# Recurrence scores level by level: interleaving, a merged first level, and the order of the steps at the stage roots

## The chip, the cores and the metric

The kernel runs on one core of one Trainium2 chip. Five engines matter here: TensorE (PE, with its weight loads PEld), VectorE (DVE), ScalarE (ACT), the DMA engines, and SyncE (SP), which issues the DMAs. The metric is the device time of one execution in microseconds (us); lower is better. Where several executions of one kernel are known, their median counts.

## The reference, cut to what matters

The model is a two-layer hybrid on one sequence of 256 tokens and 1024 channels, in float32: layer 0 is a gated linear recurrence (HGRN2), layer 1 a sparse attention (NSA), each followed by a SwiGLU feed-forward part. Only the recurrence is touched by the larger part of the change:

```python
def step(state, inp):                      # one chunk of 64 tokens, 8 heads of 128 channels
    q_, k_, v_, g_ = inp
    G = jnp.cumsum(g_, axis=2)             # running sum of log decays
    o_inter = jnp.einsum('bhtk,bhkv->bhtv', q_ * jnp.exp(G), state)
    diff = G[:, :, :, None, :] - G[:, :, None, :, :]
    decay = jnp.where(causal, jnp.exp(jnp.where(causal, diff, 0.0)), 0.0)
    attn = jnp.einsum('bhtk,bhsk,bhtsk->bhts', q_, k_, decay)
    o_intra = jnp.einsum('bhts,bhsv->bhtv', attn, v_)
    ...
    return new_state, o_inter + o_intra
...
o = rms_norm(o, out_norm) * jax.nn.silu(g)
return o @ w_out
```

What is computed per head is a causal 256 x 256 score matrix with a decay for each channel and pair of positions, times the values, then a norm over the head's 128 outputs, a gate, and an output projection.

## The kernel before

Activations lie with channels on the partitions and the 256 tokens along the free axis. Every linear layer is made of three passes on PE: the weight is split into a high and a low half (`wh` by ACT at L321, `wl` by DVE at L325), the activation likewise, and `mm3` multiplies hi by hi, hi by lo and lo by hi (L529 to L531). One *step* in the text below is one such triple of 256 columns. Weights come from HBM in blocks of 1 MB through a ring of four buffers (`raw`, issued on SP in the order of `SCHED`). `process` takes the next block and splits it; `fetch` processes ahead.

The recurrence (`hgrn`) is laid out by the list `ORDER["hgrn"]`. Its heads are handled in four pairs (i = 0 to 3), its tokens in two halves, so there are four (head, half) blocks for each pair. Tokens in `ORDER` are: `D` decays, `i`, `g`, `o` the value, gate and output products, `S` scores, `V` values, `G` and `H` gating, `x` what is left of the products between. A `+` in front makes a product a generator of steps; `S0/4` issues four steps of it behind each block of scores. The order on PE among these is fixed by `issue_after`; all else is ordered by a list scheduler of the tile framework, by program order and by when operands are expected.

- `hgrn_decays` works through eight levels b = 1, 2, 4, ..., 128. At each level ACT copies the operand tile X of the level (L1021 for b = 1, L1023 for the rest; the levels 64 and 128 go to tiles that the trace calls `s`), and DVE multiplies the running decays (L1026, L1028). Level tiles come from one pool of `XBUFS` = 14 buffers, two pairs at a time; the next two pairs' first tiles (L985) need buffers that scores have set free.
- `hgrn_scores` computes for a pair the scores: for each of its four blocks `head_scores` makes 4 diagonal products of 32 columns (L1076), 5 x 4 products of 16 columns for the levels 1 to 16 (L1082), each on a column tile of 128 x 32 of the array into `psl`, and 4 products for the levels 32 and 64 (L1088, L1092) into `psu`. A float32 product is two records in the trace. `psx` (L1049) is the block of the second half against the first. DVE then masks `psl` (L1051, L1058, L1062) and ACT copies `psu` and `psx` (L1065, L1066) into the score tile A.
- `hgrn_values` multiplies A by the values (L1108 to L1110), takes the norm (ACT L1113, then DVE, with small operations), scales (L1129), transposes on PE (L1132) and writes the result over `q` (L1133).
- `ada_pe` (L425) makes the modulation vectors with `raw` as the moving operand, also on column tiles; its result is transposed at L436 from a tile of the tag `m`.
- `stat_end` at the end of each residual (the *root* of the next stage) sums squares on PE (L713), takes a reciprocal root with Newton steps on DVE (L488 to L493), builds a diagonal `dg` (L720) and spreads it over the partitions on PE (`rb`, L722).

PSUM is shared by tags: `acc` with 3 banks, `m` with 4, `ada` with 1.

The order of the recurrence before:

```python
"D0 k i0 g0 S1 i1 +g1 S0/4 x c1 V0 D1 i2 i3 G0 +g2 +g3 +o0 S2/5 S3/5 V1 x H o1 G1 o2 o3"
```

Of the kernel before, what the change touches and what calls it, by code (L numbers as in the profile page):

```python
# [21 lines left out]
P = 128  # L22
# [8 lines left out]
XBUFS = 14  # L31
XMOD, XOFF = 5, 9
WIDE = (1,)
PTS = 3
# [20 lines left out]
def _ada_g(l):  # L55
# [9 lines left out]
        "D0 k i0 g0 S1 i1 +g1 S0/4 x c1 V0 D1 i2 i3 G0 +g2 +g3 +o0 S2/5 S3/5 V1 x H o1 G1 o2 o3"  # L65
# [134 lines left out]
class K:  # L200
# [101 lines left out]
    def process(self):  # L302
# [9 lines left out]
        if kind in ("lin", "half"):  # L312
            ws = []
            for h in range(1 if kind == "half" else 2):
# [10 lines left out]
                nc.vector.tensor_tensor(wl, u, wh.bitcast(F32), op=ALU.subtract)  # L325
# [88 lines left out]
    def ada_pe(self, kind, l, i, t):  # L414
# [19 lines left out]
        pt = self.m_tile([P, 4, P], "adat")  # L434
# [272 lines left out]
    def stat_end(self, ps=None):  # L707
# [11 lines left out]
        for tt in range(2):  # L719
            nc.vector.tensor_scalar_mul(dg[:, tt], self.c("ident"), r[:, tt:tt + 1])  # L720
# [93 lines left out]
    def hgrn(self):  # L814
# [3 lines left out]
        with self.tc.tile_pool(name="hg", bufs=1) as gp, self.tc.tile_pool(name="hg2", bufs=2) as g2:  # L818
# [19 lines left out]
            q = gp.tile([P, 8, S], F32, name="q")  # L838
# [8 lines left out]
            for i in range(4):  # L847
                self.act(q[:, 2 * i:2 * i + 2], pq[i], AF.Silu)
# [40 lines left out]
            def gate_out(n, k, gg, oh, ol):  # L889
                nc.vector.tensor_tensor(gg, q[:, 2 * n:2 * n + 2], gg, op=ALU.mult)  # L890
                self.split(oh[:, k:k + 2, :256], ol[:, k:k + 2, :256], gg)
# [32 lines left out]
            Xs = {}  # L924
            for t in ORDER["hgrn"]:
# [3 lines left out]
                elif t[0] == "D":  # L929
                    Xs.update(self.hgrn_decays(logs if n == 0 else self.hgrn_logs({m: pf[m] for m in (2, 3)}, g2), q, g2))  # L930
                elif t[0] == "S":
                    As[n] = self.hgrn_scores(Xs.pop(n), q[:, 2 * n:2 * n + 2], g2, n, between, int(t[3:] or 0))
                elif t[0] == "+":
                    between = chain(between, {"g": gate_steps, "o": out_steps, "i": value_steps}[t[1]](int(t[2])))
# [13 lines left out]
                elif t[0] == "V":  # L948
                    self.hgrn_values((2 * n, 2 * n + 1), As, v[n], g2, q)
# [44 lines left out]
    def hgrn_decays(self, logs, qs, g2):  # L994
# [16 lines left out]
        for i, rf in rfs.items():  # L1011
            nc.vector.tensor_tensor(rf[:, 0].rearrange("p (h s) -> p h s", h=2), rf[:, 2].rearrange("p (h s) -> p h s", h=2),
                                    qs[:, 2 * i:2 * i + 2], op=ALU.mult)
            nc.vector.tensor_copy(Xs[i][8], rf[:, 1].rearrange("p (h s) -> p h s", h=2))
        for l, b in enumerate(LEVELS):
            n = W // (2 * b)
            for i, rf in rfs.items():
                X = new(i, l)
                if b == 1:
                    odd = [[2, S]]  # L1020
                    nc.scalar.copy(ap(X, 1, *odd), ap(rf, 1, *odd))  # L1021
                else:
                    last = nc.scalar.copy(ap(X, 0, [b, 2], [2 * b, n], [1, b]), ap(rf, W, [b - W, 2], [2 * b, n], [1, b]))  # L1023
# [9 lines left out]
    def hgrn_scores(self, X, q, g2, i, between, fill):  # L1033
# [3 lines left out]

        psl = self.m_tile([P, 4, 112], f"psl{i}")
        psu = self.m_tile([P, 4, P], f"psu{i}")
# [628 lines left out]
```

## Time and profile before

| | |
|---|---|
| runs before (us) | 734.29 median; 733.88, 734.29, 738.5 |
| profiled execution | 736.01 us, of which the span in the trace is 734.2 us |
| PE busy | 712.4 us (97%), 5949 matmul records |
| DVE, ACT busy | 580.3 us (79%), 433.6 us (59%) |
| DMA | 172.49 MB, mean 235 GB/s |
| recurrence with its products | from about 63.5 us (last of the q and f products) to about 184 us (its root) |

The span is what the trace covers; the time of the execution has 1.8 us more around it. In the timeline a row is a run of like instructions: start, length, engine, line, operation, tiles, shape, count, and in brackets how long the engine sat idle before it and what ended that. Matmul lengths overlap, because they are pipelined; what counts for PE is the distance from one start to the next. 256 columns at 128 x 128 in the reduced format start 0.12 us apart.

### The profile page before, as it was taken

The numbers are of one execution on the slowest core, as the hardware profiler recorded it, in microseconds if no ns is written. First come the engines' busy times: TensorE is split into PE (matmuls) and PEld (weight loads), VectorE is DVE, ScalarE is ACT, GpSimd is POOL, SyncE is SP. The second block draws the span as 40 slices with busy tenths as digits, with TensorE's granted clock in tenths as the row PEclk, the third lists the DMA queues.
The fourth block names the chain that finished last, engine by engine and source line by source line (L and its number), as shares of the span: only waits on it lengthen the run. The fifth ranks groups of instructions, "written<-read, shape, count | busy, mean of one in ns | idle before, by whom it ended". The sixth has DMA issues, their size and how long they took to land.

```text
span 734.2 us, 14785 instructions
## 1 busy us (share of the span) xinstructions
PE 712.4 (97%) x5949; PEld 626.6 (85%) x5949; DVE 580.3 (79%) x1177; ACT 433.6 (59%) x849; POOL 0.4 (0%) x5
## 2 busy tenths in 40 slices
PE   7999899999999999999999999999999999999997
PEld 4998688789999999988898897555899888888886
DVE  6997877469999889989589888678689778677651
ACT  5669689347635444534469777558666565655330
POOL 0000000000000000000000000000000000000000
PEclk9999999999999999999999999999999999999999
DMA  8899873823669897988555541654654557556610
GB/s 349 323 370 370 295 285 127 320 81 149 246 232 401 296 363 284 344 314 298 224 191 208 226 170 58 229 205 169 238 192 174 207 203 278 188 214 236 247 69 22
DMA packets 27159, 172.49 MB, mean 235 GB/s; under 512 B 2897, under 2 KB 4305, under 8 KB 7250
## 3 DMA queue, kind: packets, MB, share of 16 engines
q1 hardware_dynamic: 26656, 170.80, 62.7%
q8 instruction: 47, 0.77, 0.4%
q10 hardware_dynamic: 434, 0.74, 0.3%
q14 instruction: 22, 0.18, 0.1%
HBM read 170.48 MB, written 1.05 MB: 234 GB/s over the span
## 4 chain that ended last, share of the span: by engine, by line
PE 81%; ACT 7%; DVE 5%; DMA 4%; issue 1%; SPq 0%; ACTq 0%
PE ffo L541 11%; PE ff L530 6%; PE ff L529 6%; PE ff L531 6%; PE ffo L542 6%; PE ff L541 5%; DMA raw<-in_w 3%; PE po L1546 3%; PE ff L542 2%; PE adapsss L425 2%; ACT wh L321 2%; PE ptt L1529 2%; PE s L1489 2%; DVE wl L325 1%; PE nso L529 1%
## 5 line engine op out<-in xcount | busy, mean ns | idle before, releaser
L321 ACT CAST wh<-raw 128x1024 fp32r<-128x1024 f32 x199 | 207.4, 1048 | 170.2 <-PE ffo L541 48.6
L325 DVE TENSOR_TENSOR wl<-raw,wh 128x1024 fp32r<-128x1024 f32 x199 | 242.0, 1221 | 68.8 <-ACT wh L321 68.3
L541 PE MATMUL ffo<-g,wh 128*128 128x512 f32 x352 | 123.6, 394 | 0.0
L542 PE MATMUL ffo<-g,wl 128*128 128x256 f32 x352 | 99.1, 282 | 0.0
L531 PE MATMUL ff<-hh,wl 128*128 128x256 f32 (+1 forms) x352 | 99.1, 282 | 0.0
L530 PE MATMUL ff<-hl,wh 128*128 128x256 f32 (+1 forms) x352 | 98.8, 282 | 0.0
L529 PE MATMUL ff<-hh,wh 128*128 128x256 f32 (+1 forms) x352 | 98.6, 282 | 0.0
L541 PEld LDWEIGHTS ffo<-g,wh 128*128 128x128 f32 x352 | 66.1, 188 | 15.4
L387 DVE CUSTOM_DVE_ANT_0 junk<-raw,crep 128x1024 f32<-128x1024 f32 x64 | 77.9, 1218 | 1.8 <-DMA raw<-in_w 1.6
L531 PEld LDWEIGHTS ff<-hh,wl 128*128 128x128 f32 x352 | 66.5, 189 | 0.0
L530 PEld LDWEIGHTS ff<-hl,wh 128*128 128x128 f32 x352 | 66.3, 189 | 0.1
L529 PEld LDWEIGHTS ff<-hh,wh 128*128 128x128 f32 x352 | 66.1, 189 | 0.2 <-ACT hh L731 0.2
L542 PEld LDWEIGHTS ffo<-g,wl 128*128 128x128 f32 x352 | 66.1, 188 | 0.0
L541 PE MATMUL ff<-h,wh 128*128 128x512 f32 x152 | 54.0, 394 | 0.0
L542 PE MATMUL ff<-h,wl 128*128 128x256 f32 x152 | 42.6, 281 | 0.0
L541 PEld LDWEIGHTS ff<-h,wh 128*128 128x128 f32 x152 | 28.7, 189 | 6.5
L463 ACT ACTIVATE Pt<-Pt,nm 128x128 f32<-128x128 f32 x64 | 28.2, 442 | 8.1 <-DVE nm L1498 7.9
L794 DVE SCALAR_TENSOR_TENSOR x<-ffo,mod,x 128x256 f32<-128x256 f32 x32 | 15.4, 481 | 19.6 <-PE ffo L542 19.2
L542 PEld LDWEIGHTS ff<-h,wl 128*128 128x128 f32 x152 | 28.6, 188 | 0.0
L524 ACT CAST g<-fg 128x256 fp32r<-128x256 f32 x44 | 17.8, 404 | 14.1 <-DVE fg L1169 13.1
L1494 DVE CUSTOM_DVE_ANT_0 Pt<-s,cst 128x128 f32<-128x128 f32 (+1 forms) x64 | 19.0, 351 | 4.1 <-PE s L1489 4.1
L1026 DVE TENSOR_TENSOR rf<-rf 128x512 f32<-128x512 f32 x28 | 18.3, 685 | 2.8 <-ACT X L1023 1.8
(493 smaller groups left out, 1750.2 us busy)
## 6 DMA issues: line engine op xcount, KB each, us to landing
raw<-in_w SPq DMA_DIRECT2D x153, 1024.0 KB, 5.1
raw<-in_w SPq DMA_DIRECT2D x11, 512.0 KB, 6.6
w1late<-in_w SPq DMA_DIRECT2D x2, 1024.0 KB, 6.5
x<-in_x SPq DMA_DIRECT2D x2, 512.0 KB, 5.3
out<-x SPq DMA_DIRECT2D x8, 128.0 KB, 1.9
cst<-in_cst ACTq DMA_DIRECT2D x1, 558.0 KB
rselr<-in_rsel SPq DMA_DIRECT2D x1, 256.0 KB, 3.5
w<-in_w SPq DMA_DIRECT2D x1, 128.0 KB, 3.4
```

The costliest lines, as they stand in the source:

```text
L321: r = nc.scalar.copy(wh, u)
L325: nc.vector.tensor_tensor(wl, u, wh.bitcast(F32), op=ALU.subtract)
L387: r = nc.vector.tensor_tensor_reduce(out=junk, in0=t[:, h * D:(h + 1) * D], in1=self.crep, scale=1.0, scalar=0.0, op0=ALU.mult, op1=ALU.ad ...
L463: r = nc.scalar.activation(out, in_, func, **kw)
L529: mm(ps, lhsT=wh, rhs=hh, start=first, stop=False)
L530: mm(ps, lhsT=wh, rhs=hl, start=False, stop=False)
L531: return mm(ps, lhsT=wl, rhs=hh, start=False, stop=last)
L541: mm(ps, lhsT=w[k][0], rhs=b, start=k == 0, stop=False)
L542: mm(ps[:, 0], lhsT=w[k][1], rhs=b[:, 0], start=False, stop=k == n - 1)
L1026: nc.vector.tensor_tensor(fr, fr, ap(rf, 2 * W, [1, 2], [2, n], [0, b]), op=ALU.mult)
L1494: nc.vector.tensor_tensor_reduce(out=Pt[half][:, br, o:o + n], in0=ps[half][:, br], in1=cs[:, S - n:], scale=1.0, scalar=-3e38, op0=ALU.ad ...
L1546: nc.tensor.matmul(po[64 * half:64 * half + 64, t], lhsT=w[:, half], rhs=rhs, start=n == 0, stop=n == len(steps) - 1, tile_position=(0, 64 ...
```

## The change

It has five parts.

1. **Scores level by level.** `S0/4` and `S1/4` now stand for two pairs each. For each level in order, and for each of the two pairs, the 16 products of the level over all four blocks are issued, then four steps of a gate or value product. So a stage of two pairs has 12 stretches of 16 products with four steps behind each: 24 stretches in the kernel. `psx` of both pairs comes last, in one `acc` bank.
2. **Diagonal and first level merged.** q is kept in a tile with three columns for two tokens: the two q values and, behind them, the odd token's decayed q of level b = 1. One product of 48 columns replaces the diagonal one of 32 and the first level's of 16, so 64 products (128 records) fall away, and with them the tile X of level 1: `XBUFS` goes from 14 to 12. Masks, gate and transposed results read and write with these strides.
3. **Values in two parts.** `hgrn_values` ends at the norm; scaling, transposes and the write to q move to `values_end`, which is a generator for the first two pairs (`+T0`, between `+g2` and `+g3`) and stands directly behind `V1` for the others (`T1`). `g0`, `i1`, `i3` become fillers, `o0` is one no longer.
4. **The transposes of `ada_pe`** take the bank of the tag `ada` in place of one of the tag `m`.
5. **Roots.** Six halves of weights, listed in `ROOTED`, have their `wl` subtraction on DVE ordered behind the last `dg` of the root before them.

```diff
-XBUFS = 14
+XBUFS = 12
+ROOTED = [("ffn_in0", 2, 1), ("ffn_in0", 3, 0), ("kv", 2, 0), ("kv", 4, 0), ("ffn_in1", 2, 1), ("ffn_in1", 3, 0)]
...
-        "D0 k i0 g0 S1 i1 +g1 S0/4 x c1 V0 D1 i2 i3 G0 +g2 +g3 +o0 S2/5 S3/5 V1 x H o1 G1 o2 o3"
+        "D0 k i0 +g0 +i1 +g1 S0/4 x c0 c1 V0 D1 i2 +i3 +g2 +T0 +g3 S1/4 x G0 V1 T1 o0 H o1 G1 o2 o3"
...
-                nc.vector.tensor_tensor(wl, u, wh.bitcast(F32), op=ALU.subtract)
+                r = nc.vector.tensor_tensor(wl, u, wh.bitcast(F32), op=ALU.subtract)
+                if (name, i, h) in ROOTED:
+                    self.after(r, self.last_dg)
...
-        pt = self.m_tile([P, 4, P], "adat")
+        pt = self.pp.tile([P, 4, P], F32, tag="ada", bufs=1, name="adat")
...
-            q = gp.tile([P, 8, S], F32, name="q")
+            q3 = gp.tile([P, 8, P, 3], F32, name="q")
+            q = q3[:, :, :, 0:2]
...
                 if b == 1:
-                    odd = [[2, S]]
-                    nc.scalar.copy(ap(X, 1, *odd), ap(rf, 1, *odd))
+                    odd = rf[:, 0].rearrange("p (h n two) -> p h n two", h=2, two=2)[:, :, :, 1]
+                    nc.scalar.copy(qs[:, 2 * i:2 * i + 2, :, 2], odd)
...
-        for h in range(2):
-            for tt in range(2):
+        psl = {i: self.m_tile([P, 4, 112], f"psl{i}") for i in pair}
+        psu, psx = {}, None
+        for l in range(6):
+            if l == 5:
+                psu = {i: self.m_tile([P, 4, P], f"psu{i}") for i in pair}
+            for i in pair:
+                q = q3[:, 2 * i:2 * i + 2]
                 with self.tc.issue_after(prev.ins) if prev else ExitStack():
-                    last = self.head_scores(psl, psu, X, q, h, tt)
+                    for ht in range(4):
+                        last = self.level_scores(l, psl[i], psu.get(i), Xs[i], q, ht)
                 with self.tc.issue_after(last.ins):
                     prev = None
                     for _ in range(fill):
                         prev = next(between, prev)
-            nc.tensor.matmul(psx[:, h], lhsT=X[7][:, h, 0:P], rhs=X[7][:, h, P:2 * P], start=True, stop=True)
+        psx = self.pp.tile([P, 4, P], F32, tag="acc", bufs=3, name=f"psx{pair[0]}")
...
-        for j in range(4):
+        for j in range(4 if l < 5 else 0):
             s = slice(base + 32 * j, base + 32 * j + 32)
-            nc.tensor.matmul(psl[32 * j:32 * j + 32, ht, 0:32], lhsT=X[8][:, h, s], rhs=q[:, h, s],
-                             start=True, stop=True, tile_position=(0, 32 * j))
...
+            if l:
+                b = LOW[l]
                 r = X[l][:, h, s].rearrange("p (n two b) -> p n two b", two=2, b=b)[:, :, 1, :]
+                lo, hi = 32 + 16 * l, 48 + 16 * l
+            else:
+                r = q[:, h, base // 2 + 16 * j:base // 2 + 16 * j + 16].rearrange("p n c -> p (n c)")
+                lo, hi = 0, 48
+            last = nc.tensor.matmul(psl[32 * j:32 * j + 32, ht, lo:hi], lhsT=X[l or 8][:, h, s], rhs=r, start=True,
+                                    stop=True, tile_position=(0, 32 * j))
...
+    def values_end(self, ns, pvs, r, g2, q):
...
+            yield last
```

More of the change, by code (lines that the diff above doesn't have):

```diff
@@ L923, in hgrn, with end_steps @@
             nxt = None
-            Xs = {}
+            Xs, ends = {}, {}
+            def end_steps(n):
+                yield from self.values_end(*ends[n])
             for t in ORDER["hgrn"]:
@@ L948, in hgrn @@
                 elif t[0] == "V":
-                    self.hgrn_values((2 * n, 2 * n + 1), As, v[n], g2, q)
+                    ends[n] = (2 * n, 2 * n + 1), *self.hgrn_values((2 * n, 2 * n + 1), As, v[n], g2, q), g2, q
+                elif t[0] == "T":
+                    for _ in self.values_end(*ends[n]):
+                        pass
                 elif t[0] == "G":
@@ L1011, in hgrn_decays @@
         for i, rf in rfs.items():
[L1012 to L1013 removed]
+            F4, q4 = (rf[:, e].rearrange("p (h n two) -> p h n two", h=2, two=2) for e in (2, 0))
+            nc.vector.tensor_tensor(q4, F4, qs[:, 2 * i:2 * i + 2, :, 0:2], op=ALU.mult)
             nc.vector.tensor_copy(Xs[i][8], rf[:, 1].rearrange("p (h s) -> p h s", h=2))
@@ L1048, in hgrn_scores, with hgrn_masks @@
                         prev = next(between, prev)
-            nc.tensor.matmul(psx[:, h], lhsT=X[7][:, h, 0:P], rhs=X[7][:, h, P:2 * P], start=True, stop=True)
+        psx = self.pp.tile([P, 4, P], F32, tag="acc", bufs=3, name=f"psx{pair[0]}")
+        with self.tc.issue_after(prev.ins) if prev else ExitStack():
+            for i in pair:
+                for h in range(2):
+                    X = Xs[i][7][:, h]
+                    nc.tensor.matmul(psx[:, 2 * (i - pair[0]) + h], lhsT=X[:, 0:P], rhs=X[:, P:2 * P], start=True, stop=True)
+        return {i: self.hgrn_masks(psl[i], psu[i], psx[:, 2 * (i - pair[0]):2 * (i - pair[0]) + 2], g2, i) for i in pair}
+    def hgrn_masks(self, psl, psu, psx, g2, i):
+        nc = self.nc
         ab = g2.tile([P, 4, 32], F32, tag="ab", name=f"ab{i}")
-        nc.vector.tensor_tensor(ab, psl[:, :, 0:32], self.c("m_d")[:, None, :].to_broadcast([P, 4, 32]), op=ALU.mult)
+        qk = psl[:, :, 0:48].rearrange("p a (n c) -> p a n c", c=3)
+        md = self.c("m_d").rearrange("p (n two) -> p n two", two=2)[:, None].to_broadcast([P, 4, 16, 2])
+        nc.vector.tensor_tensor(ab.rearrange("p a (n two) -> p a n two", two=2), qk[:, :, :, 0:2], md, op=ALU.mult)
         ml = self.c("m_l").rearrange("p (l j) -> p l j", l=5)
```

44 lines of the change are left out of this document (20 added, 24 removed).

## The prediction

> **What bounds the kernel now.** I read the page first, then the table of stretches over the recurrence, then PE's timeline there.
>
> ```profile
> span 734.2 us, 14785 instructions
> PE 712.4 (97%) x5949; PEld 626.6 (85%) x5949; DVE 580.3 (79%) x1177; ACT 433.6 (59%) x849; POOL 0.4 (0%) x5
> ...
> 80.50:90.50 10.00, 6.95 (x243) 3.71 (x241) 7.55 (x19) 5.79 (x10) 0.00 (x0) 0.83 0.74 279
> 90.50:109.10 18.60, 17.98 (x347) 15.82 (x347) 13.58 (x28) 14.48 (x23) 0.00 (x0) 1.00 0.83 302
> 124.50:151.60 27.10, 25.61 (x603) 21.01 (x602) 12.51 (x25) 11.81 (x19) 0.00 (x0) 1.00 0.75 274
> 151.60:166.90 15.30, 14.35 (x118) 13.66 (x117) 12.39 (x34) 8.90 (x27) 0.00 (x0) 1.00 0.37 124
> ```
>
> PE is busy for 97% of the span, so a change pays only by what PE starts sooner. The table's columns are the stretch, its length, then busy time (and count) of PE, PEld, DVE, ACT and POOL, the granted clock, the share of the DMA engines and GB/s. The stretch from 80.5 to 90.5 us stands out: PE is busy for 6.95 of 10 us, at a mean clock of 0.83. There the first scores (S1) run with no product between them. PE's timeline in it, and an undisturbed run of `adapsss` to compare with:
>
> ```profile
> 81.44 0.22 PE L1076 MATMUL psl<-q,X 128*32 128x32 f32 x4
> 81.84 0.22 PE L1076 MATMUL psl<-q,X 128*32 128x32 f32 x4
> 81.91 0.18 PE L1082 MATMUL psl<-X,X 128*32 128x16 f32 x1
> 85.14 0.21 PE L1082 MATMUL psl<-X,X 128*32 128x16 f32 x3 [3.05 <-issue]
> 85.51 2.46 PE L425 MATMUL adapsss<-raw,c 128*32 128x512 f32 x9
> 87.77 1.06 PE L425 MATMUL adapsss<-raw,c 128*32 128x512 f32 x1
> 90.46 0.39 PE L972 MATMUL hg_i<-wh,h 128*128 128x256 f32 x1
> 97.41 1.91 PE L425 MATMUL adapsss<-raw,c 128*32 128x512 f32 x14
> ```
>
> The same place in two successive score blocks is 0.40 us apart (81.44 and 81.84): 48 records in 0.40 us, or 8.3 ns each. Then PE stands from 81.91 to 85.14 with nothing to wait for but "issue", its own instructions. Behind the stall nine `adapsss` records take 2.46 us where 14 take 1.91, and one takes 1.06: the clock is lowered.
>
> What PE waits for in such a stall shows in the list of DMA queues, taken over 82 to 85.2, 104 to 106.8 and 144.4 to 147 us. In each there is one packet of the instruction queue:
>
> ```profile
> q8 instruction: 1, 0.02, 1.8%
> ...
> q8 instruction: 1, 0.02, 2.1%
> ...
> q8 instruction: 1, 0.02, 2.2%
> ```
>
> The other two stretches hold the other two stalls of this kind:
>
> ```profile
> 105.85 0.23 PE L1082 MATMUL psl<-X 128*32 128x16 f32 x8
> 106.70 0.38 PE L1082 MATMUL psl<-X 128*32 128x16 f32 x24 [0.61 <-issue]
> ...
> 145.33 0.28 PE L530 MATMUL hg_g<-h,wh 128*128 128x256 f32 x1
> 146.99 0.39 PE L531 MATMUL hg_g<-h,wl 128*128 128x256 f32 x1 [1.39 <-issue]
> ```
>
> So small products eat instructions faster than blocks of code arrive past 270 to 300 GB/s of weights.
>
> **The change, part by part.** Times are starts to starts on PE; a minus is a gain.
>
> *Term 1, the stall in S1: -3.2.* From 81.91 to 85.14. After the change every stretch of 16 products (32 records) has four steps, 12 matmuls at 0.12 us, behind it. A stretch and its filler take about 2.0 us (0.27 for 32 records at 8.3 ns, 1.43 for the filler, 0.3 for switching) and hold 44 matmuls. Before, S1 runs 44 such records in 0.37 us. With that pace a late block of code is covered.
>
> *Term 2, the lowered clock: -2.3.* From 85.14 to 90.46 are 5.3 us. At full clock the work in it is 37 score records (0.3), one pair of `adapsss` (2.0 by the undisturbed row, with its end), 32 `psu` records (0.5) and the switch back (0.2): 3.0. The rest, 2.3, follows from the stall, and from `psu` waiting for its operands, which under the new order are a level or more ahead.
>
> *Term 3, the two smaller code stalls: -1.9.* The first is 0.85 less 8 records (0.07), the second 1.66 less one matmul (0.12): 2.3. Before, a filled block is 56 records and 12 or 15 matmuls; after, 32 and 12. I keep 0.4 for a stall that is left; the ends are 0 and 2.3.
>
> [...]
>
> *Term 4, more switches: +3.4.* Each stretch of column-tiled products among full ones costs a change there and back. One of them:
>
> ```profile
> 128.66 0.28 PE L530 MATMUL hg_g<-h,wh 128*128 128x256 f32 x1
> 128.78 0.28 PE L531 MATMUL hg_g<-h,wl 128*128 128x256 f32 x1
> 128.99 0.27 PE L1076 MATMUL psl<-q,X 128*32 128x32 f32 x8
> 129.68 0.39 PE L529 MATMUL hg_g<-h,wh 128*128 128x256 f32 x1
> 129.90 0.29 PE L530 MATMUL hg_g<-h,wh 128*128 128x256 f32 x1
> ...
> 97.38 0.19 PE L1092 MATMUL psu<-X 128*32 128x32 f32 x1
> 97.39 0.62 PE L425 MATMUL adapsss<-raw,c 128*32 128x512 f32 x2
> ```
>
> From 128.78 to 129.90 are 1.12 us. Two matmuls of 0.12 and 56 records at 8.3 ns (0.47) leave 0.41, the upper end, since `psu` records are wider. The lower end is the two lengthened starts alone, 0.21 and 0.22 for 0.12: 0.19. I take 0.35, near the upper end, which holds the whole path. Before, there are 13 stretches (four for each of S0, S2, S3, and S1 as one); after, 24: 11 x 0.35 = 3.9. Beside `adapsss`, itself on column tiles, one side costs nothing (97.38 to 97.39). New filler begins with such blocks right behind a stretch about twice more often than before: -0.4, so +3.4. Ends: 11 x 0.19 = 2.1 and 11 x 0.41 = 4.5.
>
> *Term 5, the merge: -0.5.* 128 records fall away. If a record of 48 columns costs what one of 16 does, that is 128 x 8.3 ns = 1.06; if it costs as much as its two parts, 0. No row has 48 columns; I take the middle. [...] ACT and DVE lose nothing: the level-1 copy stays, only its target changes; strided reads of equal count hide beside PE.
>
> *Term 6, the weights of the first fill: -0.6.* PE waits for a block of `raw` before the first gate product:
>
> ```profile
> 73.46 1.07 PE L425 MATMUL adapsg<-raw,c 128*32 128x256 f32 x16 [1.00 <-DMA raw<-in_w]
> ```
>
> The first score stretch (0.6) now stands before it and fills a part. Ends: 0 and -1.0. Blocks are issued in the same order, and the ring's slots are freed in it, so SP's queue gets no new wait.
>
> *Term 7, new waits: +0.5.* T0 needs `o` (one buffer) twice; `psx` now holds an `acc` bank which `o0` needs while two gate products hold the others; both pairs' score tiles are ready only at the end of a stage. Ends: 0 and 2.5. Two covers decide it:
>
> ```profile
> 102.19 0.76 ACT L1021 COPY X<-rf 128x256 f32<-128x256 f32 x2
> ...
> 157.28 0.28 ACT L1113 ACTIVATE osq<-hgpv 128x128 f32<-128x128 f32 x1 [0.59 <-PE hgpv L1110]
> ...
> 166.20 0.63 ACT L524 CAST hh<-g 128x512 fp32r<-128x512 f32 x1 [0.25 <-DVE g L890]
> ```
>
> The second half's first level copies come at 102.2 before; by the terms above S1 begins at about 113, so it is covered by some 10 us. The last value product's tail, from the squares at 157.28 to the last split at 166.83, is 9.5 us; with 1.5 us (estimated) for the score tiles and 2.7 for the value products it ends 13.7 us behind `psx`. PE has in that time two steps of g3, the value products, o0 and o1 (34 steps x 0.36 = 12.2, and 2.7) and the transposes (0.9): 15.8. So it is covered by 2 us; if that were gone, each us late would be one us of the end. The `ada` bank for the transposes makes the next `adapsss` wait for DVE's read; gate blocks and score fill lie between, so 0.
>
> *Term 8, the roots: -2.2.* The wait for `dg` at the three roots that the change names:
>
> ```profile
> 184.48 0.15 DVE L716 TENSOR_SCALAR nv<-ms 128x2 f32<-128x2 f32 x1
> 188.90 1.23 DVE L325 TENSOR_TENSOR wl<-raw,wh 128x1024 fp32r<-128x1024 f32 x1 [0.33 <-ACT wh L321]
> 191.60 0.48 DVE L720 TENSOR_SCALAR dg<-cst,ny 128x128 f32<-128x128 f32 x2
> 192.14 0.70 PE L722 MATMUL rb<-dg,ones 128*128 128x256 f32 x2 [1.34 <-DVE dg L720]
> ...
> 374.31 1.22 DVE L325 TENSOR_TENSOR wl<-raw,wh 128x1024 fp32r<-128x1024 f32 x1 [0.37 <-ACT wh L321]
> 377.15 0.70 PE L722 MATMUL rb<-dg,ones 128*128 128x256 f32 x2 [0.58 <-DVE dg L720]
> ...
> 553.44 0.28 PE L529 MATMUL ff<-hh,wh 128*128 128x258 f32 x1
> 553.83 0.70 PE L722 MATMUL rb<-dg,ones 128*128 128x256 f32 x2
> ```
>
> Between `nv` and `dg` DVE puts halves of 1.23 us each. Two of them go behind `dg` at the first root (2.5 us against 1.34), one at the second (1.22 against 0.58). So PE's waits of 1.34 and 0.58, and 0.39 - 0.12 = 0.27 at the third, go: 2.2. The halves then end some 2.5 us behind `dg`, and PE has the rest of a deferred product (48 matmuls, 5.7 us) before it needs them. Ends: -2.2 and -0.6.
>
> Sum: -3.2 - 2.3 - 1.9 + 3.4 - 0.5 - 0.6 + 0.5 - 2.2 = **-6.8 us**. The profiled execution took 736.0 us (span 734.2), so it would become 729.2 and the span 727.4. Against the median of the runs, 734.3, it is **727.5 us**. What follows the recurrence is full on PE, so the gain carries to the end.
>
> **The rivals.**
>
> *Late code stays.* If blocks of code come late whatever the density, or the stalls are of another kind, terms 1 to 3 (7.4 us) do not come while the switches do: 734.3 - 6.8 + 7.4 = 734.9, slower than before. For it: in the stretches with fill the two smaller stalls exist. Against it: they cost 2.3 us there in 12 blocks, S1 alone 3.2. It decides from the point at which late code and its lowered clock cost PE 6.8 us in both stages.
>
> *The second half's levels come late.* D1 stands behind V0 in program order; filler i3, g2 and g3 is now tied behind the scores, so PE has only i2 while it waits. If D1's level chain began behind V0's norm, its first copy would come near 120 in place of 102, S1's first stretch would wait 7 us, and the clock would fall as above (2.3): 727.5 + 9.3 = 736.8. It decides from a first copy later than 113 on. Against it: ACT took D1's first operations long before V0 in the old kernel, and level buffers come free sooner.
>
> *The roots give nothing*, because the moved halves are late for the next product: 729.7.
>
> **How the numbers follow.** Forecast 0.78; late code 0.10; late levels 0.06; roots nothing 0.06. All best ends together give -3.2 - 2.3 - 2.3 + 2.1 - 1.1 - 1.0 - 2.2 = -10.0 (724.3), all worst ones about +0.5 (734.8). The likeliest case alone spans 724 to 731.5; the range for 8 in 10 is 723.5 to 733. One per cent, about what a measurement of this kernel can tell from no change, is 7.3 us, so 727.0: half a us below the forecast. Somewhat over half of the forecast's share lies below it, since the terms held back (3, 5, 6) are larger than term 7: faster 0.42. Within 1%: 0.53. Slower by over 1% needs late levels with a longer wait or both mishaps: 0.05.
>
> **What would show it.** Terms 1 and 2: no idle from "issue" over 1 us in the scores, and a granted clock of 1.00 from 63.5 us to the root. Term 4: 24 stretches with a start of 0.21 to 0.22 at both ends. Term 5: 768 score records in place of 896, the wide ones at 8 to 11 ns. Term 7: no idle over 0.5 us before the transposes, `hgpv`, o0 or o2. Term 8: no idle before `rb` at three roots. The prediction is wrong if PE waits for X, for A or for q where it now waits for code, or if a stretch costs over 0.6 us in switching.

## The result and the profile after

The changed kernel takes 728.73 us (median of six runs, 728.0 to 730.1), the kernel before 733.75 us beside it (six runs, 732.26 to 738.5). The ratio is 0.9925 with a 95% interval of 0.9897 to 0.9954: faster by 0.75%, which is within the one per cent that the prediction named as the limit of what can be told. The profiled execution took 729.42 us; before, it took 736.01. The forecast was 727.5 us, in a range from 723.5 to 733. Against the kernel before in the same group of runs the gain is 5.0 us, where 6.8 was forecast.

The page of the changed kernel begins so:

```profile
span 727.5 us, 14526 instructions
PE 714.2 (98%) x5821; PEld 627.7 (86%) x5821; DVE 578.9 (80%) x1177; ACT 433.6 (60%) x849; POOL 0.4 (0%) x5
```

There are 128 matmul records less, as the merge says, and PE is busy for 98% of a span that is 6.7 us shorter. Two rows of the table of stretches, for the two score stages of the recurrence:

```profile
71.60:99.00 27.40, 26.78 (x502) 21.65 (x494) 23.46 (x48) 23.41 (x38) 0.00 (x0) 1.00 0.92 347
111.30:138.00 26.70, 26.64 (x512) 20.85 (x512) 15.98 (x35) 15.43 (x24) 0.00 (x0) 1.00 0.66 233
```

And PE's waits over the recurrence, 62 to 176 us: who waited, for whom, the total, how often and the longest. The changed kernel's list has one line, the one before four:

```profile
PE hg_g L534 <- DVE wl L326: 0.6, 1, 0.6
```

```profile
PE psl L1082 <- issue: 3.7, 2, 3.0
PE hg_g L531 <- issue: 1.4, 1, 1.4
PE adapsg L425 <- DMA raw<-in_w: 1.0, 1, 1.0
PE hgo L529 <- DVE x L794: 0.8, 2, 0.6
```

Before, PE waited 6.9 us in that view, 5.1 of them for "issue". After, one wait of 0.6 us is left, and the granted clock is 1.00 in both stages. So the recurrence went as forecast, and better. I cut both traces at the same places of the program and took the distances between the starts of the same matmuls on PE:

| from the start of ... to ... (us) | before | after | change |
|---|---|---|---|
| first value product to the first root's `ms` (recurrence) | 120.25 | 113.31 | -6.94 |
| to the first `kv` product (first root, first feed-forward) | 185.07 | 183.30 | -1.77 |
| to the last `nq` product (second root) | 76.51 | 76.05 | -0.46 |
| to the last score of the attention, `s` | 56.36 | 57.47 | +1.11 |
| to the last `nso` matmul (attention's tail, output projection) | 42.25 | 44.98 | +2.73 |
| to the last `ffo` matmul (third root, second feed-forward) | 186.04 | 186.00 | -0.04 |

The rows sum to -5.37 us; another 1.3 us lie ahead of the first row, in the start. Those 1.3 us are scatter: over the fourteen traces of this study the first value product starts at 62.1 to 63.8 us, with the old recurrence and with the new one alike. The gain up to the last `nq` product is 9.2 us, and 3.8 us of it are given back in the attention, a stage whose arithmetic the change doesn't touch. The experiments had two questions: what earned the 6.9 us, and who gave back the 3.8.

### The profile page after: what moved, and what is told of

Same layout as the page of the kernel before. It is cut to its first block, busy times and chain, and to the rows that moved or that the text cites. A ratio compares the mean times of both kernels' runs of the same rounds, so it can differ in the third digit from the quotient of the medians.

```text
span 727.5 us, 14526 instructions
## 1 busy us (share of the span) xinstructions
PE 714.2 (98%) x5821; PEld 627.7 (86%) x5821; DVE 578.9 (80%) x1177; ACT 433.6 (60%) x849; POOL 0.4 (0%) x5
## 4 chain that ended last, share of the span: by engine, by line
PE 84%; ACT 7%; DVE 5%; DMA 2%; issue 1%; SPq 0%; ACTq 0%
PE ffo L544 11%; PE ff L533 6%; PE ff L534 6%; PE ff L532 6%; PE ffo L545 6%; PE ff L544 5%; PE po L1579 3%; PE ff L545 2%; PE adapsss L428 2%; PE ptt L1562 2%; PE s L1522 1%; PE nso L532 1%; PE hgo L532 1%; ACT wh L322 1%; PE nso L534 1%; PE nso L533 1%
```

## The experiments

Times are medians, and ratios are against the kernel before in the same group of runs (733.2 to 734.5 us).

### 1. The root's steps alone

```diff
-ROOTED = [("ffn_in0", 2, 1), ("ffn_in0", 3, 0), ("kv", 2, 0), ("kv", 4, 0), ("ffn_in1", 2, 1), ("ffn_in1", 3, 0)]
+ROOTED = []
```

> The changed kernel with an empty list ROOTED (the root's steps are no longer put ahead of the weight halves); all else as changed. Theory (each root's matmul waits for its own DVE steps): the idle times before rb come back as in the kernel before, 1.34 + 0.58 + 0.27 = 2.2 us over three roots, and the time goes from 728.7 to about 730.9. Rival (something else is late as soon as the root is early): at most 0.5 us, 728.7 to 729.2, with the time from the last ffn_out or kv product to the next product unchanged.

Measured: 730.8 us, ratio 0.9953 (0.9937 to 0.997), 2.1 us slower than the changed kernel. The waits of PE between 176 and 560 us, first without the edit of the roots, then in the changed kernel:

```profile
PE rb L725 <- DVE dg L723: 2.1, 2, 1.3
```

```profile
PE rb L725 <- DVE dg L723: 0.4, 2, 0.2
```

The waits are back, and the segments of the table go back with them: 185.26 for the second and 76.66 for the third. The third root gains nothing: the last segment is 185.87 us without the edit and 186.00 with it. The 0.39 us ahead of its `rb` in the kernel before are 0.45 in the changed kernel. So the roots are worth a little over 2 us, all of it at the first two.

### 2. The bank of `adat`

The change took `adat` from the four `m` banks into the single `ada` bank everywhere. Here it goes back for the modulations that are made during the attention:

```diff
-        pt = self.pp.tile([P, 4, P], F32, tag="ada", bufs=1, name="adat")
+        pt = self.m_tile([P, 4, P], "adat") if l in (2, 3) else self.pp.tile([P, 4, P], F32, tag="ada", bufs=1, name="adat")
```

> The changed kernel, but the adat tile of modulations 2 and 3 (those that are made during attention) is taken from the four m banks again, as before the change; that of the recurrence stays in the ada bank. Theory (the bank of adat alters which matmuls the order of the attention's tail interleaves, and this gives back about 2.5 us there): the stretch from the last score of attention to the output projection goes from 47.8 back to about 45.1 us, and the time to about 726.2. Rival (the order in the tail is set by something else that the change moved): the stretch stays at 47.8 and the time at 728.7. The 1.5 us of lowered clock in the attention may or may not stay in both.

Measured: 726.7 us, ratio 0.99 (0.9875 to 0.9924). The two attention segments are 56.35 and 42.28, those of the kernel before to 0.03 us, while the recurrence keeps its gain (113.13). PE's timeline of the tail, first of the changed kernel, then with `adat` on `m`:

```profile
503.43 0.65 PE L1579 MATMUL po<-PT,V 128*64 128x256 f32 x4
504.00 0.33 PE L1562 MATMUL ptt<-cst,Pt 128*128 128x128 f32 x1
504.26 0.43 PE L1579 MATMUL po<-PT,V 128*64 128x128 f32 x2
504.63 0.33 PE L1562 MATMUL ptt<-cst,Pt 128*128 128x128 f32 x1
504.89 0.65 PE L1579 MATMUL po<-PT,V 128*64 128x256 f32 x2
505.46 0.33 PE L1562 MATMUL ptt<-cst,Pt 128*128 128x128 f32 x1
```

```profile
502.57 1.24 PE L1579 MATMUL po<-PT,V 128*64 128x256 f32 x11
503.75 0.65 PE L1562 MATMUL ptt<-cst,Pt 128*128 128x128 f32 x4
504.33 0.43 PE L1579 MATMUL po<-PT,V 128*64 128x128 f32 x2
504.69 0.44 PE L1562 MATMUL ptt<-cst,Pt 128*128 128x128 f32 x2
```

In the changed kernel transpositions go one at a time between pairs of value products, and a single one of them holds PE for 0.26 us (504.00 to 504.26). Counted over the records from the last score to the end of `nso`, PE goes into tiled matmuls 14 times in the changed kernel, and 8 times with `adat` on `m`, as before the change; eight `adapsss` matmuls have also moved there from ahead of the last score. No row shows a wait; the matmuls only stand in another order. The two segments together went from 98.6 to 102.4 us, of which 1.5 are the clock, as the next paragraph shows. So the bank of one tile costs the attention the other 2.3 us (the medians of the two kernels differ by 2.0).

The changed kernels of experiments 1, 3 and 7 have the same order in the attention and 55.94 us in the segment before its tail, where the changed kernel has 57.47. These 1.5 us are the clock. In the table of stretches of the changed kernel, the stretch of 3.41 us in which the granted clock is lowered and the one ahead of it:

```profile
438.51:441.92 3.41, 2.95 (x9) 1.03 (x8) 3.31 (x19) 1.61 (x8) 0.00 (x0) 1.00 0.00 0
441.92:445.33 3.41, 3.41 (x18) 3.41 (x17) 2.44 (x12) 3.41 (x16) 0.00 (x0) 0.50 0.02 5
```

The kernel before has the same pattern in S1 and not here:

```profile
82.39:85.80 3.41, 0.66 (x41) 0.53 (x45) 1.65 (x6) 0.41 (x2) 0.00 (x0) 1.00 0.69 247
85.80:89.22 3.42, 3.42 (x28) 1.30 (x23) 2.77 (x9) 3.42 (x7) 0.00 (x0) 0.50 0.55 175
```

In both, the stretch ahead of the one at half clock has PE busy for less than its 3.41 us: for 2.95 us with 9 matmul records in the changed kernel, for 0.66 us with 41 in the kernel before. The clock records of these two traces put the edges on a grid of 3.413 us (441.92 - 11.84 = 126 x 3.413 and 85.80 - 14.12 = 21 x 3.413, 11.84 and 14.12 being where the first record of the clock starts). The thin place of the attention is there in the kernel before too; on its grid the slot that holds it, 447.62 to 451.03 us, has 11 records in 2.94 us, and the clock behind it is 1.00. With `adat` on `m` the slot that holds the thin place has 11 records too, where the changed kernel has 9:

```profile
437.19:440.60 3.41, 2.94 (x11) 1.18 (x8) 3.33 (x23) 1.58 (x4) 0.00 (x0) 1.00 0.00 0
440.60:444.02 3.42, 3.42 (x25) 2.73 (x24) 2.59 (x16) 3.42 (x17) 0.00 (x0) 1.00 0.02 5
```

In the fourteen traces of this study a slot at half clock lies in the attention in five: in the changed kernel, in the kernels of experiments 4, 10 and 12, and three times in that of experiment 11, which reordered the stage. The kernel of experiment 12 has the attention of the kernel before, and takes 57.85 us for the segment in place of 56.36. So the 1.5 us come and go under one order of the attention, the new as well as the old, and don't belong to the new order. That they hang on where the thin place meets the grid is my estimate from these rows; no experiment moved the grid by intent. Nor do the rows show how thin a slot has to be: in the kernel before the slot from 143.83 to 147.25 us has 16 records in 2.03 us, and the clock behind it is 1.00. The six runs of the changed kernel differ among themselves too: with one program, the mean granted clock was 1.000 in three of them and 0.998 to 0.999 in the other three, and one slot of 3.41 us at half clock takes 0.002 off the mean of such a span (1.7 of 727.5 us). Where the slots of the five runs that were not profiled lay is not on record.

### 3. Twelve stretches in place of 24

```diff
-            for i in pair:
-                q = q3[:, 2 * i:2 * i + 2]
-                with self.tc.issue_after(prev.ins) if prev else ExitStack():
+            with self.tc.issue_after(prev.ins) if prev else ExitStack():
+                for i in pair:
...
-                with self.tc.issue_after(last.ins):
-                    prev = None
-                    for _ in range(fill):
-                        prev = next(between, prev)
+            with self.tc.issue_after(last.ins):
+                prev = None
+                for _ in range(2 * fill):
+                    prev = next(between, prev)
```

> The changed kernel with both pairs of tiles of a level in one stretch, and eight product steps behind it in place of four: 12 tiled stretches in place of 24, the same matmuls. Theory (each there-and-back between tiled and full matmuls costs 0.3 to 0.4 us and nothing else is bound to the stretches): 12 x 0.33 = 4 us less, about 724.8. Rival (what the change won comes from short tiled stretches, and a stretch of 32 dense records runs out of code again): stops of 0.8 to 3 us with nothing named as the releaser come back in the scores, and the time is 729 to 733.

Measured: 725.29 us, ratio 0.9878 (0.9855 to 0.9902). The recurrence takes 110.25 us, 3.06 less than in the changed kernel, and PE's waits in it are:

```profile
PE hgt L1163 <- DVE o L1160: 0.5, 1, 0.5
PE hgpv L1135 <- ACT A L1091: 0.5, 1, 0.5
PE hg_g L534 <- DVE wl L326: 0.4, 1, 0.4
```

No stop by "issue". The waits are 0.8 us more than the 0.6 of the changed kernel, so 12 there-and-backs gave 3.06 + 0.8 = 3.9 us: 0.32 each. The forecast took 0.35.

### 4. and 5. The kernel before, with S1 in pieces

What if only S1's unbroken run was at fault? Two orders of the kernel before cut it into pieces, by one string each (everything else, scores by heads too, as before):

```diff
-"D0 k i0 g0 S1 i1 +g1 S0/4 x c1 V0 D1 i2 i3 G0 +g2 +g3 +o0 S2/5 S3/5 V1 x H o1 G1 o2 o3"
+"D0 k i0 +g0 S1/4 x c0 i1 +g1 S0/4 x c1 V0 D1 i2 i3 G0 +g2 +g3 +o0 S2/5 S3/5 V1 x H o1 G1 o2 o3"
```

```diff
-"D0 k i0 g0 S1 i1 +g1 S0/4 x c1 V0 D1 i2 i3 G0 +g2 +g3 +o0 S2/5 S3/5 V1 x H o1 G1 o2 o3"
+"D0 k i0 g0 +i1 S1/4 x +g1 S0/4 x c1 V0 D1 i2 i3 G0 +g2 +g3 +o0 S2/5 S3/5 V1 x H o1 G1 o2 o3"
```

> The kernel before, with one edit: gate product 0 runs in four parts between the heads of S1 (as gate product 1 does in S0), in place of ahead of it. No level order, no merge, no new banks, no root edit. Theory (the stop of 3.2 us in S1 and the lowered clock of 2.3 us behind it come from S1's unbroken run of scores): both go, three more there-and-backs cost 1.0, so about 733.75 - 5.5 + 1.0 = 729.2; should the lowered clock come up elsewhere, up to 731. Rival (the scores by heads run out of code wherever they stand, or the gain came from the order by levels): the stop stays or is moved, and the time is 733 to 735.

> The kernel before, with one edit: value product 1, which stood behind S1, runs in four parts between the heads of S1; gate product 0 stays ahead of S1 in one piece and covers the decays, which it no longer did in the run before this one. Theory (stop and lowered clock come from an unbroken run of scores): the stop of 3.2 and the lowered clock of 2.3 us go, three more there-and-backs cost 0.8 to 1.0, about 733.9 - 4.6 = 729.3. Rival (the order by levels is what cures it, scores by heads run out of code also in pieces): stops of 1 to 3 us stay in S1, 732 to 735.

Both missed. The first takes 745.91 us, ratio 1.0157 (1.0129 to 1.0185), the second 736.09, ratio 1.0015 (0.9998 to 1.0031). PE's waits up to 122 us in the first, and between 70 and 92 us in the second:

```profile
PE psl L1082 <- ACT X L1023: 6.5, 4, 2.4
PE psu L1088 <- ACT s L1023: 4.7, 1, 4.7
```

```profile
PE psu L1088 <- ACT s L1023: 3.1, 1, 3.1
```

The stop by "issue" of 3.0 us is gone from S1 in the second, and a wait of 3.1 us for the last level's copy stands in its place. Scores by heads need all levels of a head at once, so S1 couldn't be done before the decays were, and they were late. In the first of the two, gate product 0 no longer stands between the decays and S1, the waits add up to 11.2 us, and four slots at half clock (13.65 us) follow from 74.8 us on: the granted clock is 0.67 from 72 to 80 us and 0.65 from 80 to 92. Stops by "issue" stay in the second too, outside the window shown: four over the whole recurrence, 2.9 us in all, one of them of 1.0 us between S1's pieces.

In the kernel before, the two causes are tangled. Two rows of ACT there:

```profile
85.43 0.63 ACT L985 ACTIVATE X<-s 128x512 f32<-128x512 f32 x1 [3.00 <-PE psl L1082]
85.97 1.12 ACT L1023 COPY s<-rf 128x512 f32<-128x512 f32 x2
```

The copies of the last level start only after the stop, but ACT had itself stood for 3.00 us behind scores that the stop held up. DVE was done with the decays for these two copies (L1026, 82.60 to 83.88) before the stop ended. Without the stop, PE would have come to `psu` near 82.4 and found its operand near 84.5 (estimates: 81.91 and the 0.5 us that the rest of `psl` took behind the stop; 83.88 and a copy of 0.6). So the decays were late there too, by less than in the second order.

The changed kernel stands in the same place of the program and doesn't wait. Rows of the views of its level copies, of its scores and of its last levels, with counts, durations, and first and last start:

```profile
L1035 ACT COPY s<-rf x4: 611/616/622, 82.2 to 85.1; 128x512 f32<-128x512 f32 x4
...
L1109 PE MATMUL psl<-q,X x128: 206/206/231, 70.1 to 113.7; 128*32 128x48 f32 x128
...
L1115 PE MATMUL psu<-s x32: 219/220/243, 96.7 to 99.7; 128*32 128x64 f32 x32
```

The first scores start at 70.1, when the last level is 12 us from being copied; the last level is ready from 82.2 to 85.7 on and is used at 96.7. So the order by levels starts on the first level as soon as it is there, and runs the products while the others are made.

### 6. Both faster edits together

> Both edits that were faster alone: 12 tiled stretches in place of 24, and adat of modulations 2 and 3 in the m banks. Theory (they act at different places, so they add): from first value product to the first root 110.2, from the last score to the output projection's end 42.3, together 5.8 us under the changed kernel by the traces, about 722.9. Rival (one takes the other's cover): 724 to 726. Should a slot of lowered clock come up, 1.5 more.

The edits are those of 2 and 3. Measured: 721.89 us, ratio 0.9843 (0.9822 to 0.9863). The recurrence takes 109.71, the tail 42.30. It is the fastest kernel of the study, 1.6% faster than the kernel before, and 6.8 us faster than the changed kernel by the medians (6.0 by the two ratios, since the kernel before took 733.75 us in one group of runs and 734.46 in the other).

### 7. The merge taken back

```diff
-                r = q[:, h, base // 2 + 16 * j:base // 2 + 16 * j + 16].rearrange("p n c -> p (n c)")
-                lo, hi = 0, 48
+                r = q[:, h, base // 2 + 16 * j:base // 2 + 16 * j + 16]
+                nc.tensor.matmul(psl[32 * j:32 * j + 32, ht, 0:32], lhsT=X[8][:, h, s], rhs=r[:, :, 0:2], start=True,
+                                 stop=True, tile_position=(0, 32 * j))
+                r, lo, hi = r[:, :, 2], 32, 48
```

> The changed kernel with the merge taken back: diagonal (32 columns) and first level (16 columns) as two matmuls again, in the same stretch, 896 score matmuls in place of 768; level order and all else as changed. Theory of the prediction: 128 records at 4 to 8.3 ns, 0.5 to 1.06 us more between the first value product and the first root, 729.2 to 729.8. Rival (the matmuls that were merged lay beside others of the same row groups and cost nothing): under 0.2 us. Other rival (more records in a stretch, and the code runs out again): a stop of 0.8 us or more.

Measured: 730.26 us, ratio 0.9943 (0.9927 to 0.996). The recurrence takes 114.39 us, 1.08 more than with the merge. The four stretches that hold the first level show it directly: counted from the last full matmul ahead of them to the second one behind, they take 1.14 us more together (1.19 for 0.91 in three of them, 2.94 for 2.64 in the first, with `adapsss`). The waits are 0.4 us larger too (1.0 in the same view, against 0.6), and the rest of the recurrence is about that much shorter. Two rows of the next kernel give the price of a record: 64 of 48 columns, and then those of 16:

```profile
127.96 0.89 PE L1109 MATMUL psl<-q,X 128*32 128x48 f32 x64
128.67 1.33 PE L1109 MATMUL psl<-X 128*32 128x16 f32 x137
```

From 127.96 to 128.67 is 0.71 us for 64 records, 11.1 ns each, against 2 x 8.3 = 16.6 for the two that it replaces, if they cost what they did in the kernel before. 128 x 5.5 ns is 0.70 us. This edit issues the two products of a column tile one behind the other, where the kernel before went over all four tiles first, and its records cost about 10 ns (0.64 us for 64). So the merge is worth 0.7 us against the old order and 1.1 against this one.

### 8. S1 in one run again, by levels

```diff
-"D0 k i0 +g0 +i1 +g1 S0/4 x c0 c1 V0 D1 i2 +i3 +g2 +T0 +g3 S1/4 x G0 V1 T1 o0 H o1 G1 o2 o3"
+"D0 k i0 +g0 +i1 +g1 S0/4 x c0 c1 V0 D1 i2 +i3 +g2 +T0 x S1/0 +g3 x G0 V1 T1 o0 H o1 G1 o2 o3"
```

> The changed kernel with S1 (the level order and the merge kept) in one unbroken run of 384 scores: value product 3, gate product 2 and the transpositions are done before it, gate product 3 after it. Theory (an unbroken run of scores of 8 ns each uses up code faster than it comes, whatever the order of levels): a stop of 1 us or more with no releaser comes back inside S1; it takes back part of 11 saved there-and-backs (2.8 us at 0.26 each), 727 to 729.5. Rival (the order by levels or the merge cured the stop): no stop over 0.5 us in S1 and about 725.5 to 726.

Measured: 733.34 us, ratio 0.9989 (0.9974 to 1.0003). PE's waits between 126 and 145 us, and the queue of instructions over 130 to 133 and 134.5 to 138.9 us:

```profile
PE psu L1115 <- issue: 4.3, 1, 4.3
PE psl L1109 <- issue: 3.0, 1, 3.0
```

```profile
q8 instruction: 1, 0.02, 2.0%
...
q8 instruction: 1, 0.02, 1.5%
```

Order by levels and merge were kept, no wait for an operand is listed, and the stops are back, each with its packet of code. Two slots at half clock follow (the mean granted clock of the execution is 0.995), and the recurrence loses 4.6 us. The time lies above the forecast of 727 to 729.5, which had the stop but not its 7.3 us. So what keeps the stops away here is the filler between the scores, not their order. In the changed kernel the queue brings three such packets between 111 and 138 us, and PE waits for none.

### 9. and 10. How dense may it be?

One kernel is the kernel before, S1 behind value product 1, and pieces with two steps between them; a piece is one block of scores, 28 products or 56 records. The other is the kernel of experiment 6 with two levels of both pairs in one stretch, 64 products or 128 records, and 16 steps behind it:

```diff
-"D0 k i0 g0 S1 i1 +g1 S0/4 x c1 V0 D1 i2 i3 G0 +g2 +g3 +o0 S2/5 S3/5 V1 x H o1 G1 o2 o3"
+"D0 k i0 g0 i1 +g1 S1/2 S0/2 x c1 V0 D1 i2 i3 G0 +g2 +g3 +o0 S2/5 S3/5 V1 x H o1 G1 o2 o3"
```

```diff
-            with self.tc.issue_after(last.ins):
-                for _ in range(2 * fill):
+            if l % 2:
+                with self.tc.issue_after(last.ins):
+                    for _ in range(4 * fill):
```

> The kernel before, with the scores still head by head (all levels of a head in one stretch of 32 records), but S1 behind value product 1 and both S1 and S0 in four pieces each, with two steps of gate product 1 between pieces. The run of S1 in pieces showed a wait of 3.07 us for the last decays in place of the stop; here gate product 0 and value product 1 cover the decays. Theory (S1 stood still for two reasons that lay side by side, code and decays; with both covered the order by levels isn't needed): no stop or wait over 1 us in S1, clock 1.00, three more there-and-backs at 0.26: about 734.2 - 5.5 + 0.8 = 729.5. Rival (pieces of 32 records head by head still run out of code, or the masks and values behind them come late): 732 to 735.

> The fastest kernel so far with two levels of both pairs in one stretch (64 records) and 16 product steps behind it: 6 stretches in place of 12. Theory (0.26 us for each there-and-back, and a run of 64 records doesn't use up the code): 1.5 us less, about 720.4. Rival (the run is long enough for a stop, or the second level of a stretch waits for its decays): a stop or wait of 0.8 us or more in a stretch, 721.5 to 723.5.

Both missed in the direction of their rivals, and by more than those said: 740.72 us, ratio 1.0107 (1.0073 to 1.0142), and 728.5 us, ratio 0.9922 (0.9894 to 0.995). The longest of PE's waits in the recurrence of the first and of the second:

```profile
PE psl L1082 <- issue: 3.1, 2, 2.2
PE hgt L1132 <- DVE o L1129: 2.7, 2, 1.5
```

```profile
PE psu L1115 <- DVE ab L1084: 2.5, 1, 2.5
PE psu L1115 <- issue: 1.4, 2, 1.1
```

The waits for DVE and ACT come of the moved order and cloud both totals: by the lines named, the transpositions of the first wait for the norm of the value products, and the last levels of the second for the masks of the levels before them. What can be read is the code. Counted in products, pieces of 28 with two steps between them stop in three places, 0.6 to 2.2 us each; unbroken runs stop for 2.0 (experiment 12) to 7.3 us; stretches of 16 with four steps or 32 with eight show no such stop; but 64 with 16 stop again for 1.4 us, though full matmuls and scores are mixed in the same proportion. So it looks as if the length of a run counts beside the mean; the waits around it keep that from being settled. Whether scores by heads, as late as here and with four steps behind each block, would have done as well as the order by levels was not run.

### 11. The attention's tail in order

```diff
-                for e in range(3):
-                    nc.tensor.transpose(pt[:, e], Pt[half][:, br, e * P:(e + 1) * P], self.c("ident"))
+                with self.tc.issue_after(self.last_po.ins) if self.last_po else ExitStack():
+                    for e in range(3):
+                        tr = nc.tensor.transpose(pt[:, e], Pt[half][:, br, e * P:(e + 1) * P], self.c("ident"))
...
+                with self.tc.issue_after(tr.ins):
...
+        self.last_po = mm if j > 4 else None
```

Here `mm` is the last matmul of `po`.

> The fastest kernel so far, and in the attention every value product po waits for all transpositions of its own pair of heads (line 1562 ahead of 1579), for the last two pairs the transpositions wait for the value product before, too. Theory (the attention's tail pays for each change between full and tiled matmuls): 8 ways into tiled mode between the last score and the output projection become about 4, 1 to 1.8 us less, about 720.5. Rival (the order was interleaved because the copies out of PSUM are late otherwise): waits for DVE or ACT of 0.4 us and more ahead of po and ptt come up in its place, 722 to 725.

A miss: 734.13 us, ratio 1.0013 (0.9997 to 1.0029), 12 us slower than the kernel it was made from. The tail itself is a little shorter (41.86 for 42.30), but the 22 `adapsss` matmuls that stood in it now stand ahead of it. I tied all eight pairs and not the last ones alone, and the segment before the tail went from 56.36 to 69.38. The waits between 440 and 520 us:

```profile
PE po L1582 <- ACT PT L1569: 2.4, 1, 2.4
PE ptt L1564 <- DVE Pt L1547: 1.8, 1, 1.8
```

Three slots at half clock lie between 489 and 514 us, around these waits (the mean granted clock of the execution is 0.993). So the fine interleaving gave cover that the order by pairs doesn't; whether a tail alone could be had with fewer turns wasn't tried.

### 12. Late code without late decays

Experiment 5 showed two causes in the same place. Here S1 runs unbroken as it did, but one product later, when the decays are done:

```diff
-"D0 k i0 g0 S1 i1 +g1 S0/4 x c1 V0 D1 i2 i3 G0 +g2 +g3 +o0 S2/5 S3/5 V1 x H o1 G1 o2 o3"
+"D0 k i0 g0 i1 S1 +g1 S0/4 x c1 V0 D1 i2 i3 G0 +g2 +g3 +o0 S2/5 S3/5 V1 x H o1 G1 o2 o3"
```

> The kernel before, with S1 in one unbroken run as it was, but behind value product 1 instead of ahead of it, so that the decays are done when it starts. It tells apart the two reasons for which S1 stood still in the kernel before: late code and late decays, which the run of S1 in pieces showed to lie side by side. Theory (late code alone is enough): a stop of 2 to 4 us named issue stays in S1, no wait of S1 for ACT or DVE, lowered clock behind it, and the time stays within 2 us of the kernel before, 732 to 736. Rival (the stop was the late decays, and code is late only in their company): no stop over 1 us in S1, clock 1.00, about 734.2 - 5.5 = 728.7.

Measured: 736.46 us, ratio 1.0029 (1.0007 to 1.005). The two longest kinds of wait in the recurrence:

```profile
PE psu L1088 <- issue: 2.0, 1, 2.0
PE psl L1082 <- issue: 1.3, 1, 1.3
```

No score waits for ACT or DVE now, and the stop by "issue" stays, shorter than the 3.0 us before, with a slot at half clock behind it (the granted clock is 0.86 from 92 to 104 us). Late code alone is enough for a stop in S1; the late decays hold it where no stop by "issue" does (experiment 5). Either cure without the other leaves the kernel where it was, in these two orders.

That "issue" means code here is read from the times of the packets on queue q8, which are 16 KB each (0.77 MB in 47 packets on the page of the kernel before). In the recurrence of the seven traces that have such stops there are 20 of over 0.2 us, and each ends 2.2 to 2.6 us after a packet's start: 82.74 and 85.14 in the kernel before, 130.78 and 132.95, 136.34 and 138.87 in experiment 8, 90.98 and 93.29 here. With those 47 packets for 5949 matmuls and as many weight loads, a packet holds about 127 matmuls with their loads (an estimate, if q8 serves PE alone). By it scores of 8.3 ns use a packet up in 1.1 us, less than those 2.2; full matmuls of 0.12 us take 15.

## Why the prediction was right, and where it was not

The time is 1.2 us above the forecast, and the profiled execution took 729.4 us where 729.2 was forecast. But that closeness is luck, for errors lie under it that cancel: the recurrence gained 2.3 us more than its terms, the start was 1.3 us shorter by scatter, and the attention gave back 3.8. The worst ends as the prediction lists them add up to +0.9 us and not +0.5; the 0.4 for blocks beside `adapsss` is taken off there and not from the best ends.

*Terms 1 and 2, the stall and the clock in S1 (-5.5): right in size, half right in cause.* The waits by "issue" are gone and the clock is 1.00. Working out term 2 the prediction said that `psu` waits for its operands and that the new order has them a level ahead; it didn't see that these operands can hold S1 by themselves, for 3.1 us in experiment 5. Experiments 5 and 12 show that both had to go. What it said of the reason for late code, traffic of weights, isn't borne out: from a packet's start to the end of the stop it took about as long with 129 GB/s (2.17 us, experiment 8, 130 to 133 us) as with 410 (2.37 us, the kernel before, 144.4 to 147 us). The changed kernel has an answer to each: stretches with filler for the code, order by levels for the decays.

*Term 3, the smaller code stalls (-1.9): under-sized.* Nothing was left of the 0.4 that I kept back; 2.3 went.

*Term 4, the switches (+3.4): right.* There are 24 stretches, with starts of 0.20 to 0.21 us ahead and 0.22 to 0.23 behind (0.17 where a transpose follows). One of them, of 32 records of 16 columns:

```profile
76.92 0.28 PE L534 MATMUL hg_g<-h,wl 128*128 128x256 f32 x1
77.13 0.45 PE L1109 MATMUL psl<-X 128*32 128x16 f32 x32
77.51 0.39 PE L532 MATMUL hg_g<-h,wh 128*128 128x256 f32 x1
77.73 0.28 PE L533 MATMUL hg_g<-h,wh 128*128 128x256 f32 x1
```

From 76.92 to 77.73 is 0.81; two matmuls of 0.12 and 32 records at 8.3 ns leave 0.30. Taking half of the stretches away gave 0.32 each (experiment 3).

*Term 5, the merge (-0.5): somewhat under-sized, 0.7 to 1.1.* The wide record costs 11.1 ns (experiment 8), a little over the 8 to 11 that the prediction named. It is 2.8 ns slower than the 8.3 of the records in the kernel before, so against the old order the merge falls short of 1.06.

*Term 6, the weights of the first fill (-0.6): nearly right.* The wait for the block of `raw`, 1.0, is gone; 0.6 for `wl` has come behind it, which leaves 0.4.

*Term 7, new waits (+0.5): too high.* The list of waits names none before the transpositions `hgt`, `hgpv`, o0 or o2. Here was also a gain that no term had: `hgo` waited 0.8 us in two places for DVE's residual, L794, and doesn't any more. Why was not tested.

Together the recurrence gained 6.9 us where terms 1 to 7 gave 4.6: 0.4 of term 3, 0.5 of term 7, 0.8 of the wait not seen, and the rest in small differences of terms 4 to 6, which were not told apart.

*Term 8, the roots (-2.2): right in sum.* The table gives 1.77 + 0.46, experiment 1 takes 2.1 away. But idle time ahead of `rb` stays at two of the three roots, 0.20 us at the second and 0.17 at the third, and the third root's 0.27 didn't come.

*The step that failed* is the sentence "What follows the recurrence is full on PE, so the gain carries to the end". It took a busy PE for one that can't get slower. Of a gain of 9.2 us at the end of `nq`, 3.8 were given back. 2.3 went to the order of the attention's tail, which follows from the bank of `adat`, a part of the change that the prediction priced at 0: it looked for a wait at the `ada` bank, and looked only at the recurrence. The other 1.5 went to the slot of half clock that fell into the attention, which is in a trace with the old order of the attention too (experiment 12) and not in three with the new one (experiments 1, 3 and 7). Without these two the profiled execution would have been near 725.6 (729.42 - 3.8).

The rival of late code is refused for the changed kernel, and comes true elsewhere: with filler too thin or runs too long the stops come back, for 0.3 to 4.3 us each (experiments 8, 9, 10, 12). In the changed kernel three packets come in 27 us of scores and filler (111 to 138 us) without a wait; in the unbroken run of experiment 8 two come with stops of 3.0 and 4.3 us. The rival of late levels did not come in the second half, but experiment 4 shows what it costs where the cover is gone: 11.2 us of waits. The rival of the roots fell with experiment 1.

## What to carry to other kernels

In this recurrence a run of matmuls of 8.3 ns stood still for two reasons, its operands (3.1 us in experiment 5) and its own code (2.0 us in experiment 12), and in the kernel before the stop that named the one hid the other: take away each alone before you believe in either. Cut such a run into short stretches between large products, but no shorter than needed, since each there-and-back cost about 0.3 us; here 12 stretches beat 24, and 6 were slower again, though by other waits too. And when a tile is moved to another bank, follow every caller of that line to the end of the kernel: here the attention of a PE that is busy for 98% of the span got 2.3 us slower when its instructions were put into another order.

## What the runs showed of the hardware

Half clock (0.50 granted) came in slots of 3.41 us, and the first of them started 21 x 3.413 us behind the first clock record of the trace in the kernel before, 126 x 3.413 us behind it in the changed kernel. The slot ahead of it had 41 matmul records in 0.66 us of PE's busy time in the former and 9 in 2.95 us in the latter. Slots with 11 records in 2.94 us (the kernel before, 447.62 us; experiment 2, 437.19 us) and with 16 in 2.03 us (the kernel before, 143.83 us) had a clock of 1.00 behind them, so these rows give no threshold. The segment that holds the thin place of the attention took 57.47 us with a slot at half clock (the changed kernel) and 55.94 us without (experiments 1, 3 and 7, the same order). In the 20 stops by "issue" of over 0.2 us in the recurrence of seven traces, PE went on 2.2 to 2.6 us after a packet of 16 KB on q8 started; the longest stop took 4.3 us, with a single packet in it (experiment 8, 134.56 to 138.87 us). A turn from full matmuls to matmuls on column tiles and back cost 0.30 us in the changed kernel (76.92 to 77.73 us) and 0.32 us by experiment 3, without any wait in the records.
